# An fp32 decoder on one core: weights loaded by halves, matmuls in runs of sixteen, and three pieces of work put elsewhere

## The chip, the cores and the metric

The kernel runs on one core of a Trainium2 chip. The metric is the device time of one launch in microseconds (us). Before the change it is 2250.3 us, the median of 3 runs (2249.74 to 2252.86).

## The reference, cut to what matters

Two layers over 256 tokens of width 2048, all in fp32. The first mixes by retention (8 heads, keys of 256, values of 512), the second by native sparse attention (16 query heads on 4 key heads, three branches merged by gates); each is followed by a convolutional FFN of width 4096. Keys and values of the second layer are computed once, with a block MLP that compresses 32 tokens to one.

```python
for layer in range(2):
    xn = rmsnorm(h, norm_mix_gain[layer])
    if layer == 0:
        h = h + retention(xn, ret_w_in[0], ret_gn_gain[0], ret_w_out[0])
    else:
        shared = nsa_shared_kv(rmsnorm(h, nsa_kv_norm_gain), nsa_w_kv, ...)   # keys, values, block MLP
        h = h + nsa_attention(xn, nsa_w_q[0], nsa_w_o[0], *shared)
    h = h + conv_ffn(rmsnorm(h, norm_ffn_gain[layer]), ffn_w_in[layer], ...)
return rmsnorm(h, final_norm_gain)
# compress_blocks: blocks = windows of 32 tokens, stride 16, + pe; gelu(blocks @ w1) @ w2
# conv_ffn: u = xn @ w_in; 3-tap causal convolution; silu(a) * b; @ w_out
# retention: q, k rotated; scores = (q @ k) * decay; out normed per head, times silu(g); @ w_out
```

## The kernel before, in words

**Arithmetic.** Activations lie transposed, features on the 128 partitions and tokens along the row, 16 feature tiles for 2048 features. Every fp32 operand is taken as two parts: a rounded high part and the rest, the low part. A weight tile of 128x2048 comes from memory as one load and is split in two halves of 1024 columns (`split`, L127): ScalarE copies the half to a high part `h_...` (L131), VectorE subtracts it for the low part `l_...` (L132). A half holds eight blocks of 128x128. `feat` (L200) uses it in two loops: first eight high matmuls over 512 columns (`feat_high`, L194: the activation's high and low parts side by side), then eight low ones over 256 columns (`feat_low`, L198). The result is two blocks of 256 columns in one PSUM tile, added by `merge` (L239). `proj_tok` (L221) has the tokens on the output's partitions instead and issues three matmuls of 512 columns per feature tile and token tile (L233 to L235).

**Weights ahead of use.** `chunk_order` (L56) lists the halves in the order of their use. `weights` (L163) hands them out. Before a half is used, `split_ahead` has the next `AHEAD` = 2 halves split, and `load_ahead` (L139) has loads under way on SyncE's queue for `RAW` = 3 whole tiles of 1 MB; the split parts have `HALVES` = 3 buffers. So a load waits for the splits of the tile three earlier, and a split for the matmuls of the half three earlier. The first pieces of the kernel (L280) use the same raw buffers, 4 feature tiles each.

**Stages, in order.** Retention heads (`wA`; L327 to L403), its output (`wO`), first FFN (`wF0`, `wG0`), keys with the block MLP between them (`wKV`, `w1`; called the K stage), values (`wKVt`), gate, queries with scores and values (`wQ`), output (`wo`), second FFN (`wF1`, `wG1`), last norm. Every norm is a scale per token, applied behind the projection; its steps (`norm_scales`, L251) are placed between the matmuls of the stage's first tiles by the argument `between`: the function is called when the loop reaches those feature tiles.

**A head of the retention.** Queries and keys are rotated (L345 to L354: POOL and VectorE products and sums, `rot`), the score matmuls `sc` stand directly after the value projection (L360 to L364), and then comes the gate projection `pt_g` (L368). The head's product `po` (L377) needs the score.

**The K stage.** 16 key tiles, in the order compressed keys, selected keys, compressed values, window keys (`n` = 0 to 15). `key_end` scales them on POOL and splits them (`room`, L633 and L634, for selected and window keys). `operand` (L637) makes the parts of the second layer's normed input `xs_q`, four feature tiles after each of the first four key tiles. From `n` = 4 the steps of the block MLP (L549) stand inside the key tiles: per half of `w1` eight matmuls `ph` (L563). Its blocks are gathered by POOL (`blk`, one buffer) and split by ScalarE and VectorE (`bs`). The gate's and the attention's stages read `xs_q` afterwards.

**Order of instructions.** A scheduler moves the instructions of each engine, by dependencies and its own costs; the order in the code is not the order on VectorE, ScalarE and POOL.

Of the kernel before, what the change touches and what calls it, by code (L numbers as in the profile page):

```python
# [10 lines left out]
F32 = mybir.dt.float32  # L11
# [6 lines left out]
P = 128  # L18
# [10 lines left out]
RAW = 3  # L29
HALVES = 3  # L30
AHEAD = 2
# [24 lines left out]
def chunk_order():  # L56
# [10 lines left out]
    for l in range(2):  # L67
        if l == 1:
            w1 = [(("w1", b, ch), half) for b in range(2) for ch in range(4) for half in range(2)]
            for n, (b, h) in enumerate((b, h) for b in (0, 2, 1, 3) for h in range(HKV)):  # L70
# [13 lines left out]
        for j in range(DFF // P):  # L84
# [8 lines left out]
def decoder(ctx: ExitStack, tc: tile.TileContext, i, out, upto=99, dbg=None):  # L93
# [43 lines left out]
    held, loaded, ready = {}, deque(), deque()  # L137

    def load_ahead():  # L139
        while len({key for key, _ in loaded}) < RAW:  # L140
# [3 lines left out]
            key = unit[0]  # L144
            if unit[1] == 0:
                src = i[key[0]]
                for k in key[1:]:
                    src = src[k]
                held[key] = wpool.tile([P, 2048], F32, tag="raw", bufs=RAW,
                                       name="r_" + "_".join(str(k) for k in key))[:, :src.shape[-1]]  # L150
                nc.sync.dma_start(held[key], src)
            loaded.append(unit)

    def split_ahead(n):
        while len(ready) < n:
# [3 lines left out]
            key, half = loaded.popleft()  # L159
            src = held[key][:, half * 1024:min((half + 1) * 1024, held[key].shape[-1])]  # L160
            ready.append(((key, half), split(src, "_".join(str(k) for k in key + (half,)), src.shape[-1])))

    def weights(*key):  # L163

        for half in range(1 if key[0] == "wGate" else 2):
            split_ahead(AHEAD)
            unit, parts_ = ready.popleft()
            assert unit == (key, half)
            yield parts_
# [762 lines left out]
```

## Time and profile before

| | |
|---|---|
| median of 3 runs | 2250.3 us |
| profiled execution, its own time | 2249.65 us |
| span of the profile | 2247.8 us |
| mean granted TensorE clock | 0.997 of 2.4 GHz |
| memory traffic | 413.98 MB, mean 184 GB/s |
| PE busy | 99% |
| VectorE (DVE) busy | 65% |
| ScalarE (ACT) busy | 52% |
| GpSimd (POOL) busy | 20% |

The profile is of one execution. Matmuls are pipelined: the end of each is modelled, so successive matmuls overlap in the table, and the distance from one start to the next tells what each costs. "Busy" of PE says only that some matmul was under way.

### The profile page before, as it was taken

The numbers are of one execution on the slowest core, as the hardware profiler recorded it, in microseconds if no ns is written. First come the engines' busy times: TensorE is split into PE (matmuls) and PEld (weight loads), VectorE is DVE, ScalarE is ACT, GpSimd is POOL, SyncE is SP. The second block draws the span as 40 slices with busy tenths as digits, with TensorE's granted clock in tenths as the row PEclk, the third lists the DMA queues.
The fourth block names the chain that finished last, engine by engine and source line by source line (L and its number), as shares of the span: only waits on it lengthen the run. The fifth ranks groups of instructions, "written<-read, shape, count | busy, mean of one in ns | idle before, by whom it ended". The sixth has DMA issues, their size and how long they took to land. (4 is left out here: it accounts for less than half of the span.)

```text
span 2247.8 us, 31306 instructions
## 1 busy us (share of the span) xinstructions
PE 2216.6 (99%) x12236; PEld 1924.3 (86%) x12236; DVE 1456.9 (65%) x2038; ACT 1158.1 (52%) x1792; POOL 448.2 (20%) x473
## 2 busy tenths in 40 slices
PE   8999999999999999999999999999999999999997
PEld 7788888888888888888888887888888888888886
DVE  7655656556555577777755566678866777776444
ACT  5444444444444555555544455567655555555443
POOL 6110111101222211111122233000152111111332
PEclk9999999999999999999999999999999999999999
DMA  7455555555555555555555545633255555555553
GB/s 264 172 179 184 180 181 189 180 180 178 215 189 189 190 190 191 189 190 190 189 189 190 189 169 214 226 130 130 100 202 189 189 190 190 190 190 189 190 189 113
DMA packets 64516, 413.98 MB, mean 184 GB/s; under 512 B 6896, under 2 KB 13168, under 8 KB 15472
## 3 DMA queue, kind: packets, MB, share of 16 engines
q1 hardware_dynamic: 64368, 411.98, 52.0%
q8 instruction: 96, 1.57, 0.3%
q14 instruction: 52, 0.43, 0.1%
HBM read 409.86 MB, written 2.10 MB: 183 GB/s over the span
## 5 line engine op out<-in xcount | busy, mean ns | idle before, releaser
L194 PE MATMUL pf_F<-xs_f,h_wF 128*128 128x512 f32 x2048 | 513.5, 392 | 0.0
L132 DVE TENSOR_TENSOR l_wF<-r_wF,h_wF 128x1024 fp32r<-128x1024 f32 x256 | 314.4, 1228 | 189.1 <-ACT h_wF L131 184.2
L194 PEld LDWEIGHTS pf_F<-xs_f,h_wF 128*128 128x128 f32 x2048 | 368.2, 189 | 65.7
L131 ACT ACTIVATE h_wF<-r_wF 128x1024 fp32r<-128x1024 f32 x256 | 271.6, 1061 | 292.5 <-PE pf_F L194 286.9
L132 DVE TENSOR_TENSOR l_wA<-r_wA,h_wA 128x1024 fp32r<-128x1024 f32 x184 | 234.5, 1278 | 170.4 <-ACT h_wA L131 170.4
L131 ACT ACTIVATE h_wA<-r_wA 128x1024 fp32r<-128x1024 f32 x184 | 195.0, 1060 | 271.4 <-PE pt_v L235 109.4
L198 PEld LDWEIGHTS pf_F<-xs_f,l_wF 128*128 128x128 f32 x2048 | 279.4, 190 | 19.9
L198 PE MATMUL pf_F<-xs_f,l_wF 128*128 128x256 f32 x2048 | 285.6, 282 | 0.0
L194 PE MATMUL pf_G<-hid,h_wG 128*128 128x512 f32 x1024 | 256.4, 392 | 0.0
L132 DVE TENSOR_TENSOR l_wG<-r_wG,h_wG 128x1024 fp32r<-128x1024 f32 x128 | 157.5, 1230 | 143.5 <-ACT h_wG L131 143.5
L131 ACT ACTIVATE h_wG<-r_wG 128x1024 fp32r<-128x1024 f32 x128 | 135.5, 1059 | 160.8 <-PE pf_G L194 142.8
L470 POOL TENSOR_TENSOR u<-u,rrow_f 128x256 f32<-128x256 f32 x128 | 96.4, 753 | 609.6 <-DVE u L243 606.2
L194 PEld LDWEIGHTS pf_G<-hid,h_wG 128*128 128x128 f32 x1024 | 184.2, 189 | 32.9
L437 POOL TENSOR_TENSOR lowr<-low,hT 128x256 f32<-128x256 f32 x63 | 91.7, 1457 | 388.7 <-ACT low L428 388.7
L198 PEld LDWEIGHTS pf_G<-hid,l_wG 128*128 128x128 f32 x1024 | 139.7, 190 | 10.0
L198 PE MATMUL pf_G<-hid,l_wG 128*128 128x256 f32 x1024 | 142.8, 282 | 0.0
L194 PE MATMUL pf_O<-ys,h_wO 128*128 128x512 f32 x512 | 128.3, 392 | 0.0
L132 DVE TENSOR_TENSOR l_wO<-r_wO,h_wO 128x1024 fp32r<-128x1024 f32 x64 | 79.4, 1242 | 62.5 <-ACT h_wO L131 62.5
L194 PE MATMUL pf_A<-xs_ret,h_wA 128*128 128x512 f32 x448 | 112.8, 393 | 0.0
L194 PEld LDWEIGHTS pf_O<-ys,h_wO 128*128 128x128 f32 x512 | 92.2, 189 | 16.5
L131 ACT ACTIVATE h_wO<-r_wO 128x1024 fp32r<-128x1024 f32 x64 | 67.6, 1057 | 67.6 <-PE pf_O L194 53.5
L233 PE MATMUL pt_g<-h_wA,xs_ret 128*128 128x512 f32 x256 | 100.8, 394 | 0.0
(278 smaller groups left out, 3757.0 us busy)
## 6 DMA issues: line engine op xcount, KB each, us to landing
r_wF<-in_wF SPq DMA_DIRECT2D x128, 1024.0 KB, 4.7
r_wA<-in_wA SPq DMA_DIRECT2D x92, 1024.0 KB, 4.7
r_wG<-in_wG SPq DMA_DIRECT2D x64, 1024.0 KB, 4.7
r_wO<-in_wO SPq DMA_DIRECT2D x32, 1024.0 KB, 4.7
r_wKV<-in_wKV SPq DMA_DIRECT2D x16, 1024.0 KB, 4.8
r_wQ<-in_wQ SPq DMA_DIRECT2D x16, 1024.0 KB, 4.7
r_wo<-in_wo SPq DMA_DIRECT2D x16, 1024.0 KB, 4.7
r_w<-in_w SPq DMA_DIRECT2D x8, 1024.0 KB, 4.8
```

What stands on the lines that cost most here:

```text
L131: A.activation(hi[:, :n], src, AF.Copy)
L132: V.tensor_tensor(lo[:, :n], src, hi[:, :n].bitcast(F32), op=ALU.subtract)
L194: T.matmul(ps, hi[:, ws], x.rearrange("p a t -> p (a t)"), start=first, stop=False)
L198: T.matmul(ps[:, S:], lo[:, ws], x[:, 0], start=False, stop=last)
L233: T.matmul(ps[t], xs[:, k, 0, ts], hi[:, ws], start=k == 0, stop=False)
L437: G.tensor_tensor(lr, low, hT[:, m], op=ALU.add)
L470: G.tensor_tensor(u, u0, rrow, op=ALU.mult)
```

## The change

Five things are done at once.

1. *Weights by halves, lead of three.* Each half is loaded by itself (512 KB) into one of four buffers of 1024 columns; the split parts have four buffers instead of three, and three halves are split ahead instead of two. The first pieces use eight such raw tiles in turn.
2. *Runs of sixteen.* In `feat` the second half of a tile issues its lows first and then its highs, so that lows follow lows and highs follow the next tile's highs.
3. *Openings by two tiles.* The first two tiles of both FFNs and of the K stage go half by half: first half of tile 0, first half of tile 1, second halves. The norm's steps stand in the second halves, at feature tiles 12 and 14.
4. *Score.* In a retention head the score matmuls are issued inside the gate projection, at its feature tile 6.
5. *K stage.* `blk` has two buffers; the block MLP's `hg` shares the buffers of `bs`; the parts of `xs_q` are made during key tiles 4 to 11, two feature tiles each, issued after that tile's merge.

```diff
-RAW = 3
-HALVES = 3
-AHEAD = 2
+RAW = 4
+HALVES = 4
+AHEAD = 3
@@ chunk_order
+            yield from ((("wKV", h), half) for half in range(2) for h in range(2))
+            for n, (b, h) in list(enumerate(...))[2:]:
@@ load_ahead
-        while len({key for key, _ in loaded}) < RAW:
+        while len(loaded) < RAW:
...
+            raw = wpool.tile([P, 1024], F32, tag="raw", bufs=RAW, ...)
+            nc.sync.dma_start(raw[:, :n], src[:, half * 1024:half * 1024 + n])
@@ feat
-        for kk in range(8):
-            if between and k0 + kk in between[0]:
-                between[1]()
-            feat_high(ps, hi, ws[kk], xs[kk], k0 + kk == 0)
-        for kk in range(8):
-            feat_low(ps, lo, ws[kk], xs[kk], k0 + kk == n - 1)
+        odd = k0 // 8 % 2
+        for low in (odd, 1 - odd):
+            for kk in range(8):
+                if between and low == odd and k0 + kk in between[0]:
+                    between[1]()
+                if low:
+                    feat_low(ps, lo, ws[kk], xs[kk], False)
+                else:
+                    feat_high(ps, hi, ws[kk], xs[kk], k0 + kk == 0, k0 + kk == n - 1)
+    def proj_two(xs, keys, name, steps):
+        ps = [psum_j(f"pf_{name}{n}") for n in range(2)]
+        steps = iter(steps)
+        for half in range(2):
+            for n, key in enumerate(keys):
+                hi, lo = take(key, half)
+                feat(ps[n], hi, lo, [xs[:, half * 8 + kk] for kk in range(8)], half * 8, KT,
+                     ((14,) if n else (12,), lambda: next(steps)()) if half else None)
+        return ps
@@ retention head
-            pss = psum_a(f"sc{h}")
...
-            pg = proj_tok(xs, [("wA", h, 8 + ch) for ch in range(4)], f"g{h}")
+            def score():
+                pss = psum_a(f"sc{h}")
...
+            pg = proj_tok(xs, [("wA", h, 8 + ch) for ch in range(4)], f"g{h}", ((6,), score))
@@ FFN
-            pair = [proj(j, ab) for ab in range(2)] if j == 0 else None
+            pair = proj_two(xf, [(f"wF{l}", 0, ab) for ab in range(2)], f"F{l}_0_", (norm, norm)) if j == 0 else None
@@ block MLP
-                blk = bp.tile([P, HKV, NC_CMP, 8], F32, tag="blk", bufs=1, ...)
+                blk = bp.tile([P, HKV, NC_CMP, 8], F32, tag="blk", bufs=2, ...)
@@ K stage
-            ps = key_head(0, 0)
-            operand(0)
-            ps1 = key_head(0, 1, (4, 12), (norm, norm))
-            key_end(0, 0, ps)
-            key_end(0, 1, ps1)
-            operand(1)
+            for h, ps in enumerate(proj_two(xkv, [("wKV", h) for h in range(2)], "K0_", (norm, norm))):
+                key_end(0, h, ps)
             for h in range(2, HKV):
                 key_end(0, h, key_head(0, h))
-                operand(h)
...
                 if n == 11:
                     mlp1()
+                with tc.issue_after(last[0].ins), tc.issue_after(last[1].ins):
+                    operand(n - 4)
```

What this makes of the order of instructions is shown at three places. First TensorE in the first FFN, tile `wF0_2_0` and the one after it; `h_` and `l_` are high and low parts, the digits behind them block, gate or value side, and half. Before:

```order
L194 MATMUL pf_F0_2_0_6428<-xs_f0_4837,h_wF0_2_0_0_6392 128x512 x8
L198 MATMUL pf_F0_2_0_6428<-xs_f0_4837,l_wF0_2_0_0_6393 128x256 x8
L194 MATMUL pf_F0_2_0_6428<-xs_f0_4837,h_wF0_2_0_1_6429 128x512 x8
L198 MATMUL pf_F0_2_0_6428<-xs_f0_4837,l_wF0_2_0_1_6430 128x256 x8
L194 MATMUL pf_F0_2_1_6481<-xs_f0_4837,h_wF0_2_1_0_6451 128x512 x8
L198 MATMUL pf_F0_2_1_6481<-xs_f0_4837,l_wF0_2_1_0_6452 128x256 x8
```

and in the changed kernel:

```order
L197 MATMUL pf_F0_2_0_6696<-xs_f0_5041,h_wF0_2_0_0_6638 128x512 x8
L201 MATMUL pf_F0_2_0_6696<-xs_f0_5041,l_wF0_2_0_0_6639 128x256 x8
L201 MATMUL pf_F0_2_0_6696<-xs_f0_5041,l_wF0_2_0_1_6661 128x256 x8
L197 MATMUL pf_F0_2_0_6696<-xs_f0_5041,h_wF0_2_0_1_6660 128x512 x8
L197 MATMUL pf_F0_2_1_6751<-xs_f0_5041,h_wF0_2_1_0_6699 128x512 x8
L201 MATMUL pf_F0_2_1_6751<-xs_f0_5041,l_wF0_2_1_0_6700 128x256 x8
```

The second half's lows and highs have changed places, and equal matmuls stand in runs of sixteen. Second, VectorE in head 0 between the value and the gate projection (`t2` and `rot` are the rotation, `v` the values, `sc` the score, `l_wA_0_8_0` the low part of the first gate half). Before:

```order
L132 TENSOR_TENSOR l_wA_0_8_0_520<-r_wA_0_8_435,h_wA_0_8_0_519 128x1024
L349 TENSOR_TENSOR t2_0_0_539<-raw0_0_359,rope_90 128x512
L351 TENSOR_TENSOR rot0_0_542<-t1_0_0_538,t2_0_0_539 128x256
L352 TENSOR_TENSOR rot0_0_542<-t2_0_0_539,t1_0_0_538 128x256
L349 TENSOR_TENSOR t2_0_1_546<-raw0_1_366,rope_90 128x512
L132 TENSOR_TENSOR l_wA_0_8_1_578<-r_wA_0_8_435,h_wA_0_8_1_577 128x1024
L351 TENSOR_TENSOR rot0_1_549<-t1_0_1_545,t2_0_1_546 128x256
L352 TENSOR_TENSOR rot0_1_549<-t2_0_1_546,t1_0_1_545 128x256
L358 TENSOR_SCALAR v0_0_552<-pt_v0_0_373,rcol_ret_462 128x512
L358 TENSOR_SCALAR v0_1_558<-pt_v0_1_374,rcol_ret_462 128x512
L366 TENSOR_TENSOR sc0_569<-sc0_564,dec0_535 128x384
```

and in the changed kernel:

```order
L134 TENSOR_TENSOR l_wA_0_8_0_515<-r_wA_0_8_0_451,h_wA_0_8_0_514 128x1024
L134 TENSOR_TENSOR l_wA_0_8_1_540<-r_wA_0_8_1_469,h_wA_0_8_1_539 128x1024
L369 TENSOR_TENSOR t2_0_0_559<-raw0_0_363,rope_90 128x512
L371 TENSOR_TENSOR rot0_0_562<-t1_0_0_558,t2_0_0_559 128x256
L372 TENSOR_TENSOR rot0_0_562<-t2_0_0_559,t1_0_0_558 128x256
L369 TENSOR_TENSOR t2_0_1_566<-raw0_1_370,rope_90 128x512
L134 TENSOR_TENSOR l_wA_0_9_0_589<-r_wA_0_9_0_494,h_wA_0_9_0_588 128x1024
L371 TENSOR_TENSOR rot0_1_569<-t1_0_1_565,t2_0_1_566 128x256
L372 TENSOR_TENSOR rot0_1_569<-t2_0_1_566,t1_0_1_565 128x256
L378 TENSOR_SCALAR v0_0_572<-pt_v0_0_377,rcol_ret_480 128x512
L378 TENSOR_SCALAR v0_1_578<-pt_v0_1_378,rcol_ret_480 128x512
L134 TENSOR_TENSOR l_wA_0_9_1_607<-r_wA_0_9_1_512,h_wA_0_9_1_606 128x1024
```

Split 8_1 has moved ahead of the rotation, 9_0 into the place that 8_1 had, and the score's row comes later than the piece shown. Third, VectorE in the K stage behind key tile 4 (`pf_K2_0`; `l_w1_0_0_1` is the second half of the block MLP's first weights). Before:

```order
L243 TENSOR_TENSOR lowr_11615<-pf_K2_0_11569,low_11616 128x256
L546 TENSOR_TENSOR bs0_1_11717<-blk0_1_11647,bs0_1_11717 128x8x60
L634 TENSOR_TENSOR room_11312<-sq_11619,room_11312 128x2x128
L132 TENSOR_TENSOR l_wKV_10_0_11664<-r_wKV_10_11590,h_wKV_10_0_11663 128x1024
L132 TENSOR_TENSOR l_w1_0_0_1_11693<-r_w1_0_0_11528,h_w1_0_0_1_11692 128x1024
L132 TENSOR_TENSOR l_wKV_10_1_11706<-r_wKV_10_11590,h_wKV_10_1_11705 128x1024
L243 TENSOR_TENSOR lowr_11683<-pf_K2_1_11623,low_11684 128x256
```

and in the changed kernel:

```order
L570 TENSOR_TENSOR bs0_1_12161<-blk0_1_12085,bs0_1_12161 128x8x60
L263 TENSOR_TENSOR lowr_12045<-pf_K2_0_11997,low_12046 128x256
L134 TENSOR_TENSOR l_wKV_10_0_12074<-r_wKV_10_0_11998,h_wKV_10_0_12073 128x1024
L660 TENSOR_TENSOR room_11764<-sq_12049,room_11764 128x2x128
L268 SCALAR_TENSOR_TENSOR xs_q_11777<-hT_5038,cb_74,xs_q_11777 128x256 x2
L134 TENSOR_TENSOR l_w1_0_0_1_12102<-r_w1_0_0_1_12020,h_w1_0_0_1_12101 128x1024
L134 TENSOR_TENSOR l_wKV_10_1_12137<-r_wKV_10_1_12058,h_wKV_10_1_12136 128x1024
L263 TENSOR_TENSOR lowr_12121<-pf_K2_1_12057,low_12122 128x256
```

The split of `wKV_10_0` now stands ahead of `room`, and two parts of `xs_q` stand between `room` and the split of `w1`.

## Rows read from the trace of the kernel before

**Rows 1.** The page's busy time of TensorE, share of the span, instructions.

```profile
PE 2216.6 (99%) x12236; PEld 1924.3 (86%) x12236; DVE 1456.9 (65%) x2038; ACT 1158.1 (52%) x1792; POOL 448.2 (20%) x473
```

**Rows 2.** Windows: stretch, length, busy of PE PEld DVE ACT POOL, clock, DMA, GB/s.

```profile
0.00:33.00 33.00, 26.81 (x129) 20.95 (x129) 26.64 (x28) 19.89 (x32) 25.85 (x29) 1.00 0.77 268
55.50:64.00 8.50, 5.12 (x18) 4.01 (x17) 7.74 (x12) 2.85 (x4) 1.70 (x1) 0.80 0.38 130
1294.00:1407.00 113.00, 104.72 (x616) 90.39 (x615) 74.04 (x90) 62.86 (x87) 38.81 (x51) 1.00 0.54 196
1480.00:1600.00 120.00, 119.85 (x734) 106.00 (x733) 106.19 (x294) 88.69 (x297) 10.32 (x14) 1.00 0.34 120
```

**Rows 3.** Waits of TensorE's weight loads, 1294 to 1460 us: sum, times, longest.

```profile
PEld ph L563 <- DVE l_w L132: 5.9, 8, 1.1
PEld ph L563 <- ACT h_w L131: 2.6, 1, 2.6
PEld pf_K L194 <- DVE xs_kv L248: 2.0, 1, 2.0
PEld pf_K L194 <- ACT h_wKV L131: 1.1, 1, 1.1
```

**Rows 4.** Timeline of PE in the first FFN, three windows: start, us, instructions.

```profile
902.02 1.11 PE L198 MATMUL pf_F<-xs_f,l_wF 128*128 128x256 f32 x8
...
902.25 0.88 PE L198 MATMUL pf_F<-xs_f,l_wF 128*128 128x256 f32 x6
...
902.98 2.00 PE L194 MATMUL pf_F<-xs_f,h_wF 128*128 128x512 f32 x8
...
904.14 0.84 PE L194 MATMUL pf_F<-xs_f,h_wF 128*128 128x512 f32 x3
...
904.82 1.11 PE L198 MATMUL pf_F<-xs_f,l_wF 128*128 128x256 f32 x8
```

**Rows 5.** Timeline of PE in head 1: values, score, gate projection.

```profile
126.21 0.39 PE L233 MATMUL pt_v<-h_wA,xs_ret 128*128 128x512 f32 x1
...
130.74 0.39 PE L235 MATMUL pt_v<-h_wA,xs_ret 128*128 128x512 f32 x1
130.97 1.02 PE L362 MATMUL sc<-rot,rot 128*128 128x256 f32 x4
...
134.12 0.39 PE L235 MATMUL pt_g<-h_wA,xs_ret 128*128 128x512 f32 x1
```

**Rows 6.** Timeline in head 0: gate projection and score on PE, VectorE beside it.

```profile
55.52 0.39 PE L233 MATMUL pt_g<-h_wA,xs_ret 128*128 128x512 f32 x1
...
59.73 1.37 PE L362 MATMUL sc<-rot,rot 128*128 128x256 f32 x4 [3.38 <-DVE rot L351]
...
63.87 0.40 PE L235 MATMUL pt_g<-h_wA,xs_ret 128*128 128x512 f32 x1
...
56.97 2.28 DVE L132 TENSOR_TENSOR l_wA<-r_wA,h_wA 128x1024 fp32r<-128x1024 f32 x1
...
59.51 0.41 DVE L352 TENSOR_TENSOR rot<-t,t 128x256 f32<-128x256 f32 x1
60.03 1.41 DVE L358 TENSOR_SCALAR v<-pt_v,rcol_ret 128x512 f32<-128x512 f32 x2
```

**Rows 7.** Timeline of VectorE and PE in the K stage's opening.

```profile
1298.42 1.76 DVE L132 TENSOR_TENSOR l_wKV<-r_wKV,h_wKV 128x1024 fp32r<-128x1024 f32 x1
1300.11 0.47 DVE L248 SCALAR_TENSOR_TENSOR xs_kv<-hT,cb,xs_kv 128x256 fp32r<-128x256 f32 x1
...
1300.64 0.50 PE L194 MATMUL pf_K<-xs_kv,h_wKV 128*128 128x512 f32 x1 [1.57 <-DVE xs_kv L248]
```

**Rows 8.** Timeline of ScalarE in the K stage, the copy to `room`.

```profile
1330.69 0.42 ACT L633 ACTIVATE room<-sq 128x256 fp32r<-128x256 f32 x1 [2.03 <-POOL sq L630]
```

**Rows 9.** DMA issues: out, queue, count, KB each, median us to landing.

```profile
r_wF<-in_wF SPq DMA_DIRECT2D x128, 1024.0 KB, 4.7
...
r_first<-in_wA SPq DMA_DIRECT2D x7, 512.0 KB, 6.8
```

More of the change, by code (lines that the diff above doesn't have):

```diff
@@ L83, in chunk_order @@
                 yield from both("wo", m)
-        for j in range(DFF // P):
+        yield from (((f"wF{l}", 0, ab), half) for half in range(2) for ab in range(2))
+        for j in range(1, DFF // P):
             for ab in range(2):
@@ L143, in load_ahead @@
                 return
[L144 to L152, printed above, removed]
+            key, half = unit
+            src = i[key[0]]
+            for k in key[1:]:
+                src = src[k]
+            n = min(1024, src.shape[-1] - half * 1024)
+            raw = wpool.tile([P, 1024], F32, tag="raw", bufs=RAW, name="r_" + "_".join(str(k) for k in key + (half,)))
+            nc.sync.dma_start(raw[:, :n], src[:, half * 1024:half * 1024 + n])
+            loaded.append((unit, raw[:, :n]))
     def split_ahead(n):
@@ L158, in split_ahead, with take @@
                 return
-            key, half = loaded.popleft()
-            src = held[key][:, half * 1024:min((half + 1) * 1024, held[key].shape[-1])]
+            (key, half), src = loaded.popleft()
             ready.append(((key, half), split(src, "_".join(str(k) for k in key + (half,)), src.shape[-1])))
+    def take(key, half):
+        split_ahead(AHEAD)
+        unit, parts_ = ready.popleft()
+        assert unit == (key, half)
+        return parts_
     def weights(*key):
         for half in range(1 if key[0] == "wGate" else 2):
[L166 to L169, printed above, removed]
+            yield take(key, half)
     def act(name):
@@ L190, in mm3, with feat_high @@
         T.matmul(ps, a[0], b[1], start=False, stop=stop)
-    def feat_high(ps, hi, ws, x, first):
-        T.matmul(ps, hi[:, ws], x.rearrange("p a t -> p (a t)"), start=first, stop=False)
+    def feat_high(ps, hi, ws, x, first, last=False):
+        T.matmul(ps, hi[:, ws], x.rearrange("p a t -> p (a t)"), start=first, stop=last)
     def feat_low(ps, lo, ws, x, last):
@@ L237, in proj_tok @@
         return ps
+    last = [None, None]
     def merge(dst, ps, name):
@@ L241, in merge @@
         low = low[:ps.shape[0]]
-        A.activation(low, ps[:, S:], AF.Copy)
-        V.tensor_tensor(dst, ps[:, :S], low, op=ALU.add)
+        last[0] = A.activation(low, ps[:, S:], AF.Copy)
+        last[1] = V.tensor_tensor(dst, ps[:, :S], low, op=ALU.add)
     def parts(xs, k, src, gain):
@@ L457, in proj @@
         def proj(j, ab):
[L458 removed]
+            return proj_feat([xf], [(f"wF{l}", j, ab)], f"F{l}_{j}_{ab}")
         for j in range(DFF // P):
             cc = []
[L462 removed]
+            pair = proj_two(xf, [(f"wF{l}", 0, ab) for ab in range(2)], f"F{l}_0_", (norm, norm)) if j == 0 else None
             for ab in range(2):
@@ L533, in blocks @@
                 pe = c("pek" if b == 0 else "pev")
-                blk = bp.tile([P, HKV, NC_CMP, 8], F32, tag="blk", bufs=1, name=f"blk{b}_{ch}")
+                blk = bp.tile([P, HKV, NC_CMP, 8], F32, tag="blk", bufs=2, name=f"blk{b}_{ch}")
                 kv = kvc[b]
```

34 lines of the change are left out of this document (18 added, 16 removed).

## The prediction

> **What bounds the kernel now.** I read the page's line of TensorE first, then the busy times by stage, then the waits of TensorE's weight loads, and last the starts of single matmuls. TensorE is busy for 2216.6 us, 99% of the span [rows 1], so what can be won is its idle time and the spacing of its matmuls. The stages say where it idles [rows 2]: in the first 33 us, where VectorE is busy for 26.64 us; around 55.5 to 64 us, where PE works 5.12 of 8.5 us at a granted clock of 0.80 of the 2.4 GHz level; and in the K stage (keys and block MLP, 1294 to 1407 us), where it works 104.72 of 113 us. In the queries (1480 to 1600 us) it idles for 0.15 of 120 us. The waits of the K stage's weight loads have four causes [rows 3]. Everywhere else matmuls follow each other, and only their spacing counts: high matmuls (512 columns) and low ones (256) in runs of eight, 902.02 to 904.82 us, 2.80 us for a half tile of weights [rows 4].
>
> The profiled execution took 2249.65 us, 0.65 us under the median of the runs (2250.3). The sum is made against the former and 0.65 us is added at the end. Within 0.2% (4.5 us) I call no change: a measurement of this kernel can tell no less.
>
> **Runs of sixteen.** A run of eight lows takes 902.02 to 902.98, 0.96 us; its first two steps take 0.23 us, the other six 0.73 us, 0.122 each. In a run of eight highs the first five steps take 902.98 to 904.14, 0.232 each, the last three 0.68 us, 0.227 each [rows 4]. So it costs about 0.027 us to come from lows to highs (five steps, 0.005 each), and the first two lows after highs are about 0.007 us cheaper each. That a high step stays at 0.227 in longer runs is seen where only 512-column matmuls stand: from 126.21 to 130.74 there are 20 steps in 4.53 us [rows 5]. That a low step stays at 0.12 beyond the eighth no row shows; the six flat ones are the nearest. With the odd halves turned round, a pair of halves has one change from lows to highs where it had two: it saves 0.027 and loses about 0.008, net 0.019 us. The pairs are the keys that go through `feat`: 128 of wF, 64 of wG, 32 of wO, 16 each of wKV and wQ, 14 of wo, and 28 of wA, 298 in all (the three openings by two tiles save one change for two keys instead of two, which takes off 3). 295 x 0.019 = 5.6 us. Bounds: 8 us if the two cheap lows are not lost, 0 if the change is paid once for each half anyway. I take 5.6, since all three steps have rows.
>
> By the Trainium skill ("TensorE: Matmul & The Clock Gate", "Back-to-back issue gap") the isolated gap depends on the number of columns alone, 262 cycles for 256 and 518 for 512, which is an estimate of 0.109 and 0.216 us at 2.4 GHz. By that, the order of highs and lows is worth nothing. The trace does not agree: 0.232 after lows, 0.227 after highs.
>
> **Head 0's score.** Before, the score matmuls stand three matmuls into the gate projection and wait 3.38 us for the rotated key; the clock then falls to 0.80 on average over the stretch. From the first gate matmul (55.52) to the ninth (63.87) it takes 8.35 us [rows 6]. In head 1 the same score and eight gate matmuls take 130.97 to 134.12, 3.15 us [rows 5]. The difference is 5.2 us. After, the score comes six k later, 36 matmuls, 36 x 0.227 = 8.2 us: it is issued at 55.5 + 8.2 = 63.7, and the last rotated half was done at 59.51 + 0.41 = 59.9 [rows 6]. What is late next? VectorE splits half 9_0 ahead of that rotation in either case (its place before held 8_1, 56.97 to 59.25), and the third gate half needs it at 55.5 + 2 x 12 x 0.227 = 61.0: 1.7 us to spare. The next split comes behind the two scalings of v, 1.41 us in 60.03 to 61.4, and is done by 62.7 for a need at 63.7 plus the score. The score's own product is wanted only after the projection's 96 matmuls, 96 x 0.227 = 22 us after its start. So I count the whole 5.2 us; if one split slips behind, 4. In head 1 nothing waits there [rows 5], and a moved matmul costs the same.
>
> **K stage.** Four waits [rows 3]: 2.0 us for xs_kv, 1.1 for a weight half, 5.9 and 2.6 for the halves of the block MLP's w1. Weight loads start ahead of matmuls, so their 11.6 us are an upper bound; PE's own idle time of 113 - 104.72 = 8.3 us is the lower [rows 2]. I take the middle, 10.
> (a) At the opening VectorE finished the low part of the last xs_kv only at 1300.11 + 0.47, behind a split of 1.76 us and parts of xs_q, and PE had reached the tile's last high [rows 7]. Now the parts of xs_q are gone from there and the second halves come a half of another tile later, 2.8 us: this wait goes. The norm's first step stays about where it was (lows 4 of the third half, 2 x 2.8 + 0.5 us in).
> (b) The w1 halves are short for PE: eight matmuls of 256 columns, a run of 0.96 us [rows 4], to a whole split on ScalarE and VectorE; and each was wanted seven highs, 1.6 us, after its tile began. With three slots the high part of a key's second half had to wait for that of the tile before; ScalarE stood at `room` for a product from POOL, 2.03 us once, and all three splits queued behind it [rows 8]. Four slots and one split ahead of `room` start them earlier. Counted from the end of a tile, two xs_q parts (2 x 0.47), a split (1.76 at most) and w1's own (1.76) [rows 7], `room` (0.42) [rows 8] make 4.9 us, and a merge; the half is wanted after a tile with w1 matmuls and seven highs, 5.6 + 0.96 + 1.6 = 8.2.
> (c) `blk` in two buffers lets the second block run ahead; before, a block had to be read before POOL began the next, and the 2.6 us wait followed.
> What comes in: 16 parts of xs_q, at most 16 x 0.47 = 7.5 us of VectorE [rows 7], into a stage where it has 74.04 of 113 us; 81.6 of about 103 still fits. One place gets worse: POOL now makes blocks 2 and 3 ahead of the first selected key's product, so `room` stands some 3 us longer once, and I leave 1 us of waiting there. Net 9 us, bounds 5 and 11.6.
>
> **What I cost at nothing.** FFN openings by two tiles: no wait of PE stood there. The opening 33 us: VectorE sets the pace and its work is unchanged; smaller slots let the last two pieces load later, but they are wanted over 6 us after. Queries: VectorE has 106.19 of 120 us [rows 2] and gets no more work; if its order cost a wait, a slice of the 13.8 us must go first. Loads by halves: a slot is held from its DMA's issue until the split. Four slots at 2.8 us give 11.2 us; with 2.28 us for each of two split steps, the slowest such row [rows 6], 6.6 us remain for landing. A 1 MB load lands in 4.7 us; the row the other way is that of the first pieces' 512 KB, 6.8 us, in runs of 1 KB or less where the new halves have 4 KB [rows 9]. I go by the former, whose rows are as long. I take no cost.
>
> By the Trainium skill ("DMA: Bandwidth & Descriptors", "Measured (HBM→SBUF, 128 partitions, SWDGE, issued from GpSimd)") loads should be batched to at least 1 MiB for three quarters of the peak. That speaks against halving them; the fourth rival below is what it would do here.
>
> **Sum.** 5.6 + 5.2 + 9 = 19.8 us; 2249.65 - 19.8 = 2229.85, and with 0.65 the median comes to 2230.5 us. Its own range: 2226 to 2235.
>
> **Rivals.**
> 1. The order of highs and lows is worth nothing (a change is paid at each half's first wait, or lows slow down beyond the eighth): 2230.5 + 5.6 = 2236. For it: no run of sixteen lows in the trace. Against: 0.227 through 20 steps with waits at each half. Above 0.122 + 0.019 / 8 a step for lows 9 to 16, the gain is gone.
> 2. The K stage keeps its waits, since VectorE with xs_q in it stays behind or `room` moves them elsewhere: 2239.5. For it: its in-order chain over three engines; against: 21 us of free VectorE time.
> 3. Both of these and half of head 0: 2250.3 - 2.6 = 2248, no change.
> 4. Slower: weights land late. From 6.6 us of landing each further us stretches the period by 0.25 us for 756 halves (596 through `feat`, 144 of the token-wise projections, 16 of w1), 190 us; it passes break-even at 6.7. At 7 us: 0.1 x 756 = 76, 2306 us. For it: the 6.8 us row; against: the DMA share is 0.54 in the K stage and 0.34 in the queries [rows 2], and 4.7 us for twice the bytes.
>
> **How the numbers follow.** Forecast 0.64, rival 1 0.11, rival 2 0.10, rival 3 0.07, rival 4 0.04, and 0.04 for more gain than I count (to 2225: 8 + 5.2 + 11.6 = 24.8). Faster: 0.64 + 0.11 + 0.10 + 0.04 = 0.89; same 0.07; slower 0.04. The range takes in rivals 1 and 2 and the upper bounds: 2224 to 2240.
>
> **What would show it.** Right: a pair of halves at 5.57 us instead of 5.59 in the FFN, with highs in runs of sixteen; no idle PE between 55 and 64 us and a granted clock of 1.00 there; PE's idle time in the K stage under 2 us, with no wait for xs_kv or h_w. Wrong: lows at 0.13 or more late in a run; a wait of PE for a weight half whose own DMA landed last; VectorE over 95% busy in the K stage.

## The result, and the profile after

The changed kernel takes 2232.1 us, the median of 5 runs (2231.4 to 2233.37), against 2250.3 us: ratio 0.9919, 95% interval 0.9908 to 0.993, 18.2 us less. The forecast was 2230.5 us, in a range of 2224 to 2240. The profiled execution took 2232.05 us, its span is 2230.3 us, 17.5 us under that of before.

Where the 17.5 us came from, by the starts of each stage's first matmul in the two traces, in us ("runs" in the last column: a share of the 5.6 us forecast for the runs of sixteen):

| stage | before | after | difference | forecast |
|---|---|---|---|---|
| start of the program to the values of head 0 | 32.63 | 33.20 | +0.57 | 0 |
| values of head 0 to first queries of head 1 | 53.34 | 48.01 | -5.33 | -5.2 |
| rest of the heads, output | 671.09 | 670.34 | -0.75 | runs |
| both FFNs | 1073.97 | 1070.16 | -3.81 | runs |
| K stage | 112.14 | 103.85 | -8.29 | -9 |
| values, gate | 56.37 | 55.90 | -0.47 | in the above |
| queries | 136.06 | 136.41 | +0.35 | runs |
| output of the second layer | 97.58 | 97.36 | -0.22 | runs |
| last norm and output | 14.61 | 15.04 | +0.43 | 0 |

Windows of the changed kernel, columns as in [rows 2]; the two last are its K stage and its queries:

```profile
0.00:33.00 33.00, 26.95 (x127) 21.15 (x128) 26.74 (x27) 19.34 (x31) 25.90 (x30) 1.00 0.74 249
55.50:64.00 8.50, 8.50 (x40) 7.02 (x39) 8.25 (x12) 3.70 (x5) 1.73 (x1) 1.00 0.20 69
1286.60:1390.50 103.90, 101.57 (x614) 90.26 (x613) 79.86 (x95) 65.45 (x96) 46.41 (x51) 1.00 0.64 210
1446.40:1582.80 136.40, 136.10 (x827) 120.07 (x825) 116.81 (x310) 97.84 (x309) 12.29 (x18) 1.00 0.37 121
```

PE no longer idles between 55.5 and 64 us, and the granted clock there is 1.00 instead of 0.80. The 0.80 was one stretch of 3.4 us at 1.2 GHz (0.50) in the trace of before, behind PE's wait of 3.38 us:

```profile
60.40:63.80 3.40, 3.40 (x12) 2.87 (x11) 2.85 (x6) 1.78 (x3) 0.00 (x0) 0.50 0.75 295
```

In the K stage PE's idle time has fallen from 8.3 us [rows 2] to 2.3. VectorE does 79.86 us of work in 103.9 there, as the forecast had it (81.6 of about 103).

PE in the first FFN (start, us, instructions), as in [rows 4]:

```profile
900.68 3.82 PE L197 MATMUL pf_F<-xs_f,h_wF 128*128 128x512 f32 x16
904.34 2.08 PE L201 MATMUL pf_F<-xs_f,l_wF 128*128 128x256 f32 x16
906.25 0.63 PE L197 MATMUL pf_F<-xs_f,h_wF 128*128 128x512 f32 x2
```

Sixteen highs take 3.66 us and sixteen lows 1.91, 0.119 each: a tile in 5.57 us, as forecast, where two halves took 2 x 2.80. The lows do not slow down beyond the eighth, and the first five highs behind sixteen lows take 0.232 us each, as behind eight.

Head 0, timeline of PE and VectorE:

```profile
64.18 1.02 PE L385 MATMUL sc<-rot,rot 128*128 128x256 f32 x4
65.04 0.61 PE L387 MATMUL sc<-rot,rot 128*128 128x128 f32 x4
...
60.04 0.41 DVE L372 TENSOR_TENSOR rot<-t,t 128x256 f32<-128x256 f32 x1
...
61.89 1.21 DVE L134 TENSOR_TENSOR l_wA<-r_wA,h_wA 128x1024 fp32r<-128x1024 f32 x1
```

The rotation ends at 60.45, the score starts at 64.18 without a wait, where it waited 3.38 us [rows 6].

The waits of the weight loads in the K stage that are left, as in [rows 3]:

```profile
PEld ph L587 <- DVE l_w L134: 1.8, 2, 1.1
PEld ph L587 <- ACT h_w L133: 1.5, 1, 1.5
```

The wait for xs_kv is gone. What is left has one main cause; the timeline around it, engine by engine:

```profile
1315.30 6.22 POOL L563 TENSOR_TENSOR blk<-kvc,cm 128x120 f32<-128x120 f32 x8 [2.02 <-DVE bs L570]
1321.48 0.75 POOL L656 TENSOR_TENSOR sq<-lowr,rrow_kv 128x256 f32<-128x256 f32 x1
...
1322.27 0.42 ACT L659 ACTIVATE room<-sq 128x256 fp32r<-128x256 f32 x1 [4.98 <-POOL sq L656]
1322.59 0.90 ACT L267 ACTIVATE xs_q<-hT,cb 128x256 fp32r<-128x256 f32 x2
1323.39 1.04 ACT L133 ACTIVATE h_w<-r_w 128x1024 fp32r<-128x1024 f32 x1
...
1324.48 0.38 PE L587 MATMUL ph<-h_w,bs 128*120 128x256 f32 x1 [1.09 <-ACT h_w L133]
1325.74 0.38 PE L587 MATMUL ph<-l_w,bs 128*120 128x256 f32 x1 [0.88 <-DVE l_w L134]
```

It reads from the top: POOL makes the gathers of blocks 2 and 3 before the product of key tile 4; ScalarE stands at `room` for that product for 4.98 us; two parts of xs_q and the split of w1 stand behind it; PE loses 2.4 us, counted by its starts.

### The profile page after: what moved, and what is told of

Its sections match the earlier page's. It is cut to its first block, busy times and chain, and to the rows that moved or that the text cites. A ratio compares the mean times of both kernels' runs of the same rounds, so it can differ in the third digit from the quotient of the medians.

```text
span 2230.3 us, 32138 instructions
## 1 busy us (share of the span) xinstructions
PE 2208.3 (99%) x12236; PEld 1924.6 (86%) x12236; DVE 1516.5 (68%) x2038; ACT 1151.8 (52%) x1792; POOL 458.1 (21%) x473
## 4 chain that ended last, share of the span: by engine, by line
PE 97%; DVE 1%; POOL 1%; ACT 1%; DMA 1%; issue 0%; SPq 0%; DVEq 0%; ACTq 0%
PE pf_F L197 21%; PE pf_F L201 11%; PE pf_G L197 10%; PE pf_G L201 5%; PE pf_O L197 5%; PE pf_A L197 5%; PE pf_O L201 3%; PE pf_W L197 3%; PE pt_v L252 3%; PE pt_g L252 3%; PE pt_v L251 3%; PE pt_g L253 3%; PE pt_g L251 3%; PE pt_v L253 3%; PE pf_Q L197 3%; PE pf_A L201 2%
## 5 line engine op out<-in xcount | busy, mean ns | idle before, releaser
L197 PE MATMUL pf_F<-xs_f,h_wF 128*128 128x512 f32 x2048 | 489.2, 391 | 0.0
L134 DVE TENSOR_TENSOR l_wF<-r_wF,h_wF 128x1024 fp32r<-128x1024 f32 x256 | 338.2, 1321 | 81.1 <-ACT h_wF L133 66.0
L134 DVE TENSOR_TENSOR l_wA<-r_wA,h_wA 128x1024 fp32r<-128x1024 f32 x184 | 244.7, 1333 | 138.4 <-ACT h_wA L133 138.4
L201 PEld LDWEIGHTS pf_F<-xs_f,l_wF 128*128 128x128 f32 x2048 | 263.1, 191 | 10.1
L201 PE MATMUL pf_F<-xs_f,l_wF 128*128 128x256 f32 x2048 | 266.9, 283 | 0.0
L197 PE MATMUL pf_G<-hid,h_wG 128*128 128x512 f32 x1024 | 244.6, 391 | 0.0
L201 PEld LDWEIGHTS pf_G<-hid,l_wG 128*128 128x128 f32 x1024 | 131.3, 191 | 5.0
L201 PE MATMUL pf_G<-hid,l_wG 128*128 128x256 f32 x1024 | 132.8, 283 | 0.0
L461 POOL TENSOR_TENSOR lowr<-low,hT 128x256 f32<-128x256 f32 x63 | 49.3, 783 | 392.3 <-ACT low L452 392.3
L197 PEld LDWEIGHTS pf_O<-ys,h_wO 128*128 128x128 f32 x512 | 94.0, 188 | 18.2
L496 ACT ACTIVATE c<-u,cb 128x256 f32<-128x256 f32 x128 | 77.4, 605 | 58.0 <-POOL u L494 58.0
```

The costliest lines, as they stand in the source:

```text
L134: V.tensor_tensor(lo[:, :n], src, hi[:, :n].bitcast(F32), op=ALU.subtract)
L201: T.matmul(ps[:, S:], lo[:, ws], x[:, 0], start=False, stop=last)
L461: G.tensor_tensor(lr, low, hT[:, m], op=ALU.add)
L496: A.activation(ct, u, AF.Identity, bias=c(cbias, m, 1), scale=c(cw, 3 * m + 2, 1))
```

## The experiments

Each is an edit of the changed kernel (median 2232.1 us) and was timed against the kernel before on the same chip, whose median was 2249.4 to 2250.7 us in the three sets: `f9`, `u_blk1`, `raw2` and `u_1mb` stand in the set with 2249.4, so their medians are some 1 us low beside the others. Stage times are worked out as in the table above, from the one profiled execution, which need not be the median one. Two limits on reading them: the K stage differs by 1.2 us between the changed kernel and `u_score`, whose VectorE, ScalarE and POOL have the same instructions in the same order there; and in `u_order`, `u_lead` and `u_blk1` the granted clock in the K stage fell to 1.2 GHz for 3.4 us behind waits of PE (1.00 and 0.88 us; 2.53; 2.40 and 0.88). In this order:

```profile
1383.90:1387.30 3.40, 3.40 (x15) 3.30 (x16) 3.03 (x7) 1.58 (x4) 0.48 (x1) 0.50 0.62 180
1326.70:1330.10 3.40, 3.40 (x14) 2.72 (x13) 3.40 (x5) 2.62 (x5) 0.91 (x1) 0.50 0.63 176
1326.70:1330.10 3.40, 3.11 (x13) 3.02 (x14) 3.40 (x6) 2.61 (x6) 0.91 (x1) 0.51 0.58 154
```

By my estimate each such stretch costs 1.7 us: in `u_order` matmuls of 256 columns start 0.213 us apart in it where they start 0.120 apart outside. The changed kernel's trace has none before its last norm (2215 us).

**Runs undone** (`u_order`).

```diff
-        odd = k0 // 8 % 2
+        odd = 0
```

> The changed kernel with the runs of sixteen undone: both halves of a tile issue their eight highs first and then their eight lows. Theory (each change from lows to highs costs 0.027 us over the next five steps, each change from highs to lows gives 0.008 back): 295 pairs x 0.019 = 5.6 us come back, 2237.7 us, and a pair in the first FFN takes 5.59 us again instead of 5.57. Rival (the gain came with the lead of three and the openings, not with the order): no change, within 2 us of 2232.1. Second rival (the order also changes what VectorE and ScalarE can finish in time, since the low part of an odd half is wanted eight steps earlier with runs of sixteen): the K stage's waits for w1 change by over 1 us.

2238.88 us, ratio 0.9951 (0.9939 to 0.9964), 6.8 us slower; the profiled run is the longest of the five, 2240.69. Outside the K stage the traces give back exactly what the runs had brought: both FFNs +3.81, heads and output +0.75, second layer's output +0.20, the queries -0.36: 4.4 us. The FFNs take their old time with their openings by two tiles left in, so the openings bring nothing there. The K stage takes 3.9 us more. 1.7 of them are the lower clock (estimate), 1.5 are idle time of PE (3.8 us where the changed kernel has 2.3), and 0.3 would be the runs, by the FFN's price; the rest is open. The waits of the weight loads:

```profile
PEld ph L587 <- DVE l_w L134: 3.8, 4, 1.1
PEld ph L587 <- ACT h_w L133: 1.7, 3, 1.4
```

and the two ahead of the lower clock:

```profile
1382.61 0.38 PE L587 MATMUL ph<-h_w,bs 128*120 128x256 f32 x1 [1.00 <-ACT h_w L133]
1383.87 0.57 PE L587 MATMUL ph<-l_w,bs 128*120 128x256 f32 x1 [0.88 <-DVE l_w L134]
```

So the theory holds at 4.4 us instead of 5.6. For the second rival, that the order also sets when w1's halves are late, there are these 1.5 us, which is hardly more than the K stage differs by itself: it is not settled.

**Runs of one** (`alt`).

```diff
-        for low in (odd, 1 - odd):
-            for kk in range(8):
...
+        for kk in range(8):
+            feat_high(...)
+            feat_low(...)
```

> The changed kernel with runs of one: in every half, for each of its eight blocks, the high matmul and at once its low one. Theory of the prediction (each change from lows to highs costs 0.027 us and each from highs to lows gives 0.008 back, wherever it stands): a half has eight such changes where the changed kernel has half a one, 7.5 x 0.019 = 0.14 us, times some 590 halves = 84 us slower, 2316. Rival (a single low between two highs is too short to cost the five dearer steps; only a long run of lows makes a debt that the next highs pay): the gate projection, which stands in this order in both kernels with 48 columns of weights, takes 5.53 us for 16 pairs, 0.346 a pair, against 0.120 + 0.227 + 0.019 / 16 = 0.348 in runs of sixteen: 590 x 8 x 0.002 = some 10 us faster, 2222.

2239.77 us (2229.65 to 2241.17), ratio 0.9946 (0.9931 to 0.9961). Neither theory: not +84 us and not -10. Windows for the tiles `pf_F` in the two FFNs (PE with its count of matmuls, then PEld, DVE, ACT):

```profile
800.00:900.00 100.00, 100.00 (x579) 88.19 (x578) 7.52 (x18) 6.55 (x18) 1.00 0.57 190
1800.00:1900.00 100.00, 100.00 (x568) 86.67 (x567) 7.53 (x18) 6.57 (x18) 1.00 0.57 187
```

The same code at the same granted clock does 579 matmuls per 100 us in one FFN and 568 in the other; the mean steps are 0.2300 and 0.1167 us for a high and a low there, 0.2360 and 0.1173 here, 0.3467 and 0.3533 a pair. Runs of sixteen make 0.348 in both. So the 0.027 us are not a price of each change from lows to highs; they were seen behind runs of eight and of sixteen lows. The second FFN as a whole takes 9.95 us more than the first. Five of the six executions took 2239 to 2241 us and one 2229.65, 9.98 less than the profiled one; that would fit an execution with the cheaper pace in both FFNs, but it was not traced. What sets the pace is open.

**Score put back** (`u_score`).

```diff
-            pg = proj_tok(..., f"g{h}", ((6,), score))
+            score()
+            pg = proj_tok(..., f"g{h}")
```

> The changed kernel with the score matmuls put back directly behind the value projection in all eight heads. Theory: head 0 waits again for the rotated key, 3.4 us without a matmul and then some 2 us at half the clock, 5.2 us, 2237.3 us; the granted clock of 55.5 to 64 us falls below 0.9 again; the other heads cost the same. Rival (with three halves split ahead VectorE reaches the rotation earlier): the wait is under 2 us and the clock stays at 1.00, 2234 us or less.

2238.76 us, ratio 0.9948 (0.9935 to 0.996), 6.7 us slower. The profiled run, the shortest of the five at 2237.13, shows the wait and no lower clock, where both were expected:

```profile
60.41 1.10 PE L385 MATMUL sc<-rot,rot 128*128 128x256 f32 x4 [3.37 <-DVE rot L371]
```

The stretch of head 0 is 3.6 us longer, and the K stage 1.2 us, without a change to its code. The granted clock from 55.5 to 64 us is 1.00 here and 0.80 before, after nearly the same wait: so the slow matmuls behind it do not always come. They are the other 1.7 of the 5.3 us by which head 0 had been longer before the change. Whether they came in the longer runs no trace shows; the mean granted clock on record, 0.997 in the profiled run and 0.995 in the longest (2239.8 us), speaks for a lower clock somewhere in that one.

**Three buffers, lead of two** (`u_lead`).

```diff
-HALVES = 4
-AHEAD = 3
+HALVES = 3
+AHEAD = 2
```

> The changed kernel with split parts in three buffers and two halves split ahead, as before the change; loads by halves in four slots, runs of sixteen and the rest stay. Theory: in FFN, retention and queries nothing waits (a split of 1.06 + 1.32 us fits into the 2.8 us of a half), but in the K stage the split of w1 can begin only when the half before it is used up, so waits of 0.3 to 1.1 us come back at most w1 halves: 4 to 6 us slower, 2236 to 2238, all of it between the first key tile and the values. Rival (the fourth buffer is not needed; the K stage gained by the moved parts and the second gather buffer): under 1.5 us. Second rival: an odd half now starts with its lows, so its low part is wanted 1.9 us sooner than before the change; with a lead of two the FFN waits too, over 20 us.

2239.99 us, ratio 0.9955 (0.9943 to 0.9967), 7.9 us slower: K stage +5.8, second layer's output +0.9, second FFN +0.6, and head 0 +1.7, where the gate's second half is late as soon as the score no longer stops PE:

```profile
59.09 0.50 PE L252 MATMUL pt_g<-l_wA,xs_ret 128*128 128x512 f32 x1 [0.71 <-DVE l_wA L134]
```

The size in the K stage is the theory's, 4 to 6 us, but 1.7 of it are the lower clock (estimate), and the waits are not where it had them. PE's weight loads wait less for the halves of w1 than in the changed kernel (1.2 us, there 3.3) and 6.3 us for halves of key tiles, there none; what is late is the next half of a key tile, whose split now stands behind `room` itself:

```profile
1323.14 0.42 ACT L659 ACTIVATE room<-sq 128x256 fp32r<-128x256 f32 x1 [5.00 <-POOL sq L656]
...
1324.26 1.04 ACT L133 ACTIVATE h_wKV<-r_wKV 128x1024 fp32r<-128x1024 f32 x1
...
1325.35 2.22 PE L197 MATMUL pf_K<-xs_kv,h_wKV 128*128 128x512 f32 x7 [2.53 <-ACT h_wKV L133]
```

So the longer lead is worth some 4 us in the K stage: it takes the key halves out of the queue behind `room`. The run shows more: with the short lead the score's move brings 3.7 us in head 0 and not 5.3. In steady FFN tiles nothing waits, so the second rival falls.

**Parts of xs_q back at the first four tiles** (`u_operand`).

```diff
             for h, ps in enumerate(proj_two(...)):
                 key_end(0, h, ps)
+                operand(2 * h)
+                operand(2 * h + 1)
...
-                with tc.issue_after(last[0].ins), tc.issue_after(last[1].ins):
-                    operand(n - 4)
```

> The changed kernel with the parts of xs_q made again behind the first four key tiles, four feature tiles each, with no order forced on them; opening by two tiles, four buffers and the rest stay. Theory: in the opening VectorE and ScalarE have up to 8 parts more before the last xs_kv part, so a wait of 1 to 2 us for xs_kv comes back there; behind, the split of w1 is no longer queued behind two parts (0.9 us), so the wait at the second half of w1 shrinks by that: net 0 to +1 us, 2232 to 2233. Rival (the opening by two tiles alone removes the wait, the moved parts are a cost): 1 us faster, 2231.

2232.0 us, ratio 0.9918 (0.9905 to 0.9932): the same. No wait for xs_kv comes back; the opening has a wait of 0.7 us for the norm's scale instead, and the waits for w1 are 0.4 us shorter (2.9 for 3.3). So the moved parts brought nothing. The wait for xs_kv is gone in `u_lead` too, with the short lead; that leaves the opening by two tiles as its likely cure, but no run undid that opening by itself.

**One gather buffer** (`u_blk1`).

```diff
-                blk = bp.tile(..., tag="blk", bufs=2, ...)
+                blk = bp.tile(..., tag="blk", bufs=1, ...)
```

> The changed kernel with one gather buffer instead of two for the block MLP. Theory: with one buffer POOL can't run ahead, so the product of key tile 4 doesn't stand behind 6.2 us of gathers and that wait (2.4 us) goes; but each block's split then has to be done before the next gather, and ph waits once for the first blocks, as it did before the change (2.6 us): net within 1 us, 2231 to 2233. Rival (the second buffer is worth the 2.6 us that the prediction gave to it): 2234.7 or more.

2237.55 us, ratio 0.9945 (0.9932 to 0.9957), 5.5 us slower; in the trace the K stage takes 4.4 us more, 2.7 of idle time of PE and 1.7 of the lower clock (estimate). The rival holds with its 2.6 us, since one buffer does not bring the product forward:

```profile
1320.17 2.62 POOL L563 TENSOR_TENSOR blk<-kvc,cm 128x120 f32<-128x120 f32 x4 [2.40 <-DVE bs L570]
1322.74 0.74 POOL L656 TENSOR_TENSOR sq<-lowr,rrow_kv 128x256 f32<-128x256 f32 x1
...
1323.52 0.42 ACT L659 ACTIVATE room<-sq 128x256 fp32r<-128x256 f32 x1 [3.34 <-POOL sq L656]
...
1324.64 1.04 ACT L133 ACTIVATE h_w<-r_w 128x1024 fp32r<-128x1024 f32 x1
```

The gather now waits 2.40 us for the block before it, and the product still stands behind it.

**Gathers behind the product** (`f_blocks`).

```diff
+                with tc.issue_after(product[0].ins):   # latest key product on POOL
                     for h in range(HKV):
                         ... G.tensor_tensor(blk[:, h], win, ...)
```

> The changed kernel with one thing added: the block MLP's gathers on POOL are issued behind the latest key product on POOL, so that POOL makes the product of key tile 4 before the gathers of blocks 2 and 3 (6.22 us of POOL). Theory: ScalarE's copy to room waits 4.98 us for that product in the changed kernel, and the split of w1's second half is queued behind it; PE loses 1.25 + 1.14 us there. With the order forced this goes: 2.4 us, 2229.7 us. Rival (the gathers then come late and ph waits for the blocks, or another instruction takes room's place in the queue): the wait moves, 2231.5 to 2233.

2235.95 us, ratio 0.9935 (0.9923 to 0.9948), 3.9 us slower. My theory fell:

```profile
1319.86 0.42 ACT L662 ACTIVATE room<-sq 128x256 fp32r<-128x256 f32 x1 [2.22 <-POOL sq L659]
...
1321.83 1.12 ACT L572 ACTIVATE bs<-blk 128x480 fp32r<-128x480 f32 x1 [0.74 <-POOL blk L566]
1322.85 1.04 ACT L133 ACTIVATE h_w<-r_w 128x1024 fp32r<-128x1024 f32 x1
```

`room` comes 2.7 us earlier, counted from the stage's first matmul, but now the split of w1 queues behind `bs`, which waits for the later gather. The split itself comes only 0.8 us earlier, and PE still idles 1.2 us there, where it was 2.0. The loss comes at the blocks behind, in the same way:

```profile
1336.23 1.13 ACT L572 ACTIVATE bs<-blk 128x480 fp32r<-128x480 f32 x1 [2.53 <-POOL blk L566]
1337.26 1.05 ACT L133 ACTIVATE h_w<-r_w 128x1024 fp32r<-128x1024 f32 x1
...
1339.66 0.38 PE L590 MATMUL ph<-l_w,bs 128*120 128x256 f32 x1 [0.92 <-DVE l_w L134]
```

Over the K stage PE idles 5.2 us instead of 2.3. To move POOL's product alone only moves the wait, as the rival had it, at a higher price.

**Split of w1 ahead of room** (`f5`), **and only the fourth gathers behind the product** (`f8`).

```diff
+                    def copy():            # room, was issued in key_end
+                        A.activation(kall[0][:, h, :, at], u1, AF.Copy)
+                        V.tensor_tensor(kall[1][:, h, :, at], ...)
+                    later.append(copy)
...
+                ps = key_head(b, h, ...)
+                rest()                     # earlier tile's copy and xs_q, issue_after(latest split)
+                key_end(b, h, ps)
+                later.append(lambda n=n: operand(n - 4))
# f8 in addition, around the gathers of block ch:
+                with tc.issue_after(product[4 + 8 * b].ins) if ch == 3 else nullcontext():
```

> The changed kernel with one thing added: in the K stage the copies to room and the two parts of xs_q of a key tile are issued on ScalarE and VectorE behind the next but one split of w1, instead of ahead of it. POOL's order is left alone, so room still waits for the product behind 6.2 us of gathers. Theory: the wait of 1.25 + 1.14 us at the second half of w1 goes, since the split no longer stands behind room; what is late next is the second half of key tile 6, whose split now stands behind room and whose lows are wanted at its start, 0.8 us: net 1.5 us faster, and 0.5 at the later wait for w1, 2230.1. Rival (as in the kernel with forced gathers, another instruction takes its place and the waits for w1 stay): within 0.7 us of 2232.1 or slower.

> The kernel f5 (copies to room and parts of xs_q behind the next split of w1), and of POOL's gathers only those of the fourth block of each side are issued behind the product of key tile 4 (12 on the value side), so that this product waits for one gather of 3.1 us and not for two. Theory: room comes 3.1 us earlier and nothing queues behind it any more, all of 2.9 us of waiting goes, 2229.2. Rival (POOL's order is not what makes the time once the split of w1 stands ahead): the same as f5 within 0.4 us. Second rival: the fourth block comes late, a wait of ph for bs, over 2232.

f5: 2231.29 us, ratio 0.9916 (0.9903 to 0.9929); f8: 2229.29 us (2228.91 to 2229.63), ratio 0.9907 (0.9894 to 0.992). The runs of f5 (2230.43 to 2232.56) overlap with those of the changed kernel (2231.4 to 2233.37), so its 0.8 us are not shown to be a gain; f8 lies below both. In f5 the split comes 5.4 us ahead of `room`, and the next key half is late instead, as expected:

```profile
1317.03 1.06 ACT L135 ACTIVATE h_w<-r_w 128x1024 fp32r<-128x1024 f32 x1 [0.48 <-PE ph L589]
1322.46 0.42 ACT L663 ACTIVATE room<-sq 128x256 fp32r<-128x256 f32 x1 [4.37 <-POOL sq L658]
...
1325.94 0.50 PE L203 MATMUL pf_K<-xs_kv,l_wKV 128*128 128x256 f32 x2 [1.15 <-DVE l_wKV L136]
```

In f8 no wait of PE is left in the K stage; the stage takes 100.75 us instead of 103.85. The reason was not quite mine: `room` comes 1.5 us earlier than in f5, counted from the stage's first matmul, not 3.1, since there the four gathers ahead of the product take longer (5.64 us for 4, where f5 has 7.15 for 8).

```profile
1315.53 5.64 POOL L568 TENSOR_TENSOR blk<-kvc,cm 128x120 f32<-128x120 f32 x4 [2.02 <-DVE bs L575]
1321.13 0.75 POOL L661 TENSOR_TENSOR sq<-lowr,rrow_kv 128x256 f32<-128x256 f32 x1
```

**Queries in runs of eight, on top of f8** (`f9`).

```diff
-                    feat(ps, hi, lo, [...], half * 8, KT)
+                    feat(ps, hi, lo, [...], half * 8, KT, turned=False)   # odd = 0
```

> The kernel f8 with one thing added: in the sixteen queries both halves issue highs first again (runs of eight), the rest of the kernel keeps its runs of sixteen. Theory: in the queries other matmuls stand between the two halves, so the order brought nothing there, and the first one is late for ScalarE's and VectorE's row work: 136.41 us with it, 136.05 without (the kernel with the order undone everywhere); 0.35 us faster, 2228.9, the best of all. Rival (the 0.35 us are chance): 2229.3.

2227.89 us (2227.7 to 2228.42), ratio 0.9903 (0.9889 to 0.9916), the best of all: 4.2 us under the changed kernel by the medians, 3.6 by the ratios. The queries take 136.07 us again. (Of its 1.4 us over f8 this explains 0.3; in the traces a further 0.6 lies in the opening and head 0, whose code is the same, and the two sets differ by 1.3 us in the kernel before.)

**Two raw buffers** (`raw2`) **and whole tiles in two buffers** (`u_1mb`).

```diff
-RAW = 4
+RAW = 2
# u_1mb in addition: raw tiles of [P, 2048], one load per tile, as before the change
```

> The changed kernel with two raw buffers of 512 KB instead of four. Theory (the prediction's fourth rival as a formula: a slot is held from the issue of its load until the split's end): 3.8 us of landing + 1.06 + 1.32 of the split = 6.2 us, against 2 x 2.79 = 5.6 that two slots give; each half is stretched by 0.3 us, 756 x 0.3 = 230 us slower, 2460. If so, four slots had 4 x 2.79 - 6.2 = 5 us to spare. Rival (the 3.8 us are time in the queue behind other loads, and a load by itself lands in about 2.5 us): no stretch in the FFN, some 10 to 20 us from the K stage, whose w1 halves come at half the distance: 2245.

> The changed kernel with loads of whole tiles again (1 MB), in two buffers of 2048 columns, which take the room of the four of 1024; runs, lead and the rest stay. Theory (a load has 5.6 us from the split that frees its slot to the first split that needs it, and lands in 4.7): FFN, retention and queries keep their times within 0.5 us each; in the K stage a tile of w1 holds one of the two slots over two key tiles, so each key tile waits for its own load, 3 to 4 us at 11 tiles: 30 to 45 us slower, 2265 to 2275. Rival (a load of 1 MB uses the memory better, as the Trainium skill says of batches of 1 MiB, page DMA: Bandwidth & Descriptors, section Measured (HBM→SBUF, 128 partitions, SWDGE, issued from GpSimd)): FFN faster, and the loss in the K stage under 10 us. Second rival (with two slots the loads are late everywhere): over 100 us slower.

raw2: 2522.26 us, ratio 1.121 (1.1194 to 1.1225). The first projection of the first FFN (wF) takes 410.3 us instead of 357.0, 0.42 us for each of 128 halves where 0.3 was worked out; ScalarE's splits wait for the DMA (waits in the window of 600 to 1100 us):

```profile
ACT h_wF L133 <- DMA r_wF<-in_wF: 31.2, 41, 3.4
```

A slot is held for 2 x (2.79 + 0.42) = 6.4 us then, by my estimate; four slots give 11.2, so 4.8 us were to spare. The rival's 2245 us fell. u_1mb: 2288.46 us, ratio 1.0171 (1.0156 to 1.0187). Heads from the second on, FFNs and outputs keep their times to 0.01 us, so the second rival falls; the K stage takes 146.7 us, values and gate 70.7 instead of 55.9:

```profile
PEld pf_K L198 <- ACT h_wKV L133: 26.2, 10, 5.0
```

That is 56 us where 30 to 45 were expected: the theory counted waits at the key tiles alone and left out values and gate (14.8 us) and the granted clock, 0.88 on average in this K stage. The loads' size as such moves nothing in the other stages; in the K stage, as I read it, halves gain because a waiting half of w1 holds a quarter of the raw room, where a tile of it holds a half. (The kernel before had three buffers of 1 MB, half as much room again, which no run kept beside the other changes.) The Trainium skill's advice of batches of 1 MiB ("DMA: Bandwidth & Descriptors", "Measured (HBM→SBUF, 128 partitions, SWDGE, issued from GpSimd)") has no price here: 512 KB land in 3.8 us and 1 MB in 4.7 in the FFN, both ahead of need.

## Why the prediction was right, point by point

- **The sum**: 19.8 us forecast, 17.5 between the traces and 18.2 between the medians. By terms the traces differ from it by -1.2 (runs), +0.1 (score), -0.2 (K stage with the values), -0.6 (opening) and -0.4 (last norm).
- **Runs of sixteen**, 5.6 us forecast: 4.4 us by `u_order`. The size per pair is right in the FFNs (3.81 us over 192 pairs, 0.0198 us). It is smaller in the heads and the two outputs (0.95 us over 74 pairs, 0.013 each, the reason open), and the queries were counted with a gain and lose 0.35 us: other matmuls stand between their two halves, and `f9` has the time back without the runs there. Lows beyond the eighth stay at 0.12, which no row had shown. The reading behind it, a price of each change, fell with `alt`; for runs of eight and of sixteen both readings give the same, so the forecast did not suffer from it. Rival 1 fell with `u_order`. So did, for this stream, what it shares with the Trainium skill ("TensorE: Matmul & The Clock Gate", "Back-to-back issue gap"), whose isolated gap goes by the columns alone.
- **Head 0's score**, 5.2 us: 5.3, of which 3.6 are the wait and 1.7 the lower clock behind it. The second part was in the trace of before and did not come in that of `u_score`, so that the whole 5.3 came out is partly luck of the trace. That 1.7 us of them need the lead of three is shown by `u_lead`; the prediction's sum has that only in the third half being in time by 1.7 us.
- **K stage**, 9 us: 8.3, and 0.5 in the values behind. Here two errors made up for each other. `f8`, without a wait of PE, takes 100.75 us where the kernel before takes 112.14: without the 0.3 us of runs all the waits cost 11.1 us, near the prediction's upper bound of 11.6 and not the middle, 10. And what was left over cost 3.1 us where I left 1: the place at `room` and its cause were right, but two parts of xs_q and a split stood behind it. Of the three reasons, (b), lead and slots, is worth some 4 us by `u_lead`, though at the key halves and not at w1's, and (c), the gather buffer, 2.7 by `u_blk1`, both without the lower clock. So rival 2 fell. For (a) the wait did go, but moving xs_q had no share in it (`u_operand`), and the opening by two tiles was not undone by itself.
- **Signs**: the pair at 5.57 us and the busy PE in head 0 came. The third did not come whole: PE idles 2.3 us in the K stage, not under 2, and one wait for h_w of 1.5 us stays.
- **At nothing**: FFN openings right. The opening costs 0.6 us in the table, 0.5 of it in one split on VectorE (1.15 us at 8.07, before 0.69 at 8.03); this stretch differs by over 1 us between traces of the same code, so it is no effect of the change that I could show.
- **Loads by halves**: right. Rival 4 (2306 us) and rival 3 (no change) fell with the 18.2 us. The formula for late landing sized `raw2` at 230 us where 290 were measured.

## What to carry to other kernels

Where one engine is busy for 99%, look for what its spacing and its few waits cost, each in its own stage, and add them up; that came to within 2 us here (19.8 forecast, 18.2 measured), though part of it by errors that made up for each other. When a wait goes, follow the in-order queue of the engine that served it: the late thing is mostly not the slow instruction but a short one queued behind a wait for a third engine. To move that short one ahead (`f5`) or to hurry the third engine (`f_blocks`) each only moved the wait; the two together, with only the gathers that are not wanted at once held back, took it away (`f8`). A lead and a move can be worth their whole gain only together. And before a difference between two traces is put down to an edit, look whether the granted clock fell in one of them: 3.4 us at 1.2 GHz made up 1.7 us of `u_lead`'s and `u_blk1`'s loss.

## What was not expected of the hardware

- Alternating 512- and 256-column matmuls run at two paces, 0.3467 and 0.3533 us a pair, at a granted clock of 1.00 in both; the cheaper is below the 0.348 of long runs.
- A wait of 3.4 us on PE was followed by 3.4 us at 1.2 GHz in the trace of before and by none in `u_score`. Waits of 1.00 and 0.88 us, one behind the other, were followed by them in `u_order` (1383.9 us), waits of 1.09 and 0.88 us not in the changed kernel (1324 to 1326 us).
- POOL's gathers of 128x120 take from 0.43 to 2.69 us each in these traces (2.00 and 5.64 us for four in `f8`), and VectorE's splits of wF take 1.32 us on average after the change, 1.23 before, at the same size.
